# A hybrid attention and recurrence block: the recurrence's values projected for row blocks 4 to 7 first, and two kinds of transfer tied behind the next copy

## The chip, the cores and the metric

The kernel runs on one core of one Trainium2 chip. The metric is the time of one execution on the device in microseconds (us), the median over several runs. A core has five engines that run their own instruction queues side by side: TensorE (PE) for matmuls, VectorE (DVE), ScalarE (ACT), GpSimd (POOL) and SyncE (SP), which here only issues transfers. DMA transfers are issued from the queues of ACT, SP and POOL, and an issue stands in its queue like any other instruction.

## The reference

Input x has 1024 rows of 1024 channels, in float32. What the block computes, cut to what matters:

```python
u = rmsnorm(x, norm1_g) @ w_in
q_sb, k_sb, v_sb, f_raw, i_hg, q_hg, g_hg, gate_sb, gate_hg = split(u)
o_sb = stick_breaking_attention(q_sb, k_sb, v_sb)      # 8 heads of 64, strictly causal
f = lb + (1 - lb) * sigmoid(f_raw)                     # forget gate, per channel
k_hg = (1 - lb) * sigmoid(-f_raw)
# recurrence, 4 heads of 128: S_t = diag(f_t) S_{t-1} + k_t v_t^T, o_t = S_t^T q_t
o_hg = hgrn2_chunkwise(silu(q_hg), k_hg, i_hg, log(f)) # i_hg: the values v_t
o_hg = rmsnorm(o_hg, hg_norm_g) * silu(g_hg)
merged = sigmoid(gate_sb + b) * (o_sb @ w_o_sb) + sigmoid(gate_hg + b) * (o_hg @ w_o_hg)
h = x + merged @ w_out
h = h + square(relu(rmsnorm(h, norm2_g) @ w_ff1)) @ w_ff2
return rmsnorm(h, final_g)
```

In the attention, weight A[t,s] is sigmoid(z_ts) times the product of (1 - sigmoid(z_tj)) over the positions j between s and t.

## The kernel before

Every float32 operand of a matmul is split into a high part (a cast on ACT, line 156) and a low part (a subtraction on DVE, line 161), and each product is made of three matmuls: high by high, high by low, low by high. In the program's names the letters h and l behind a tile's name are these parts (wih and wil are those of the weights wi). All matmuls come from line 128, transposes from line 131. SBUF holds a pool of 40 tiles ("slots") of 128 x 1024 that the stages take in turn, and PSUM gives eight banks.

A scheduler orders the instructions of each engine from the data dependences and a cost model; the program's text sets priorities (`open_block`) and not the final order. `after(ins, earlier)` gives it one more rule, that `ins` is issued behind `earlier`, without making it wait for that instruction's end by a semaphore. A stream `st` of projection work (each job is some hundred matmuls that don't depend on what is under way) is dealt out between the steps of the attention, and later of the recurrence, so that TensorE has work while ACT and DVE do theirs.

**Attention.** Per head, the query blocks of 128 rows run in the order 7, 0, 6, 1, 5, 2, 4, 3. For each, TensorE makes z, ACT two activations of it (rm at line 804, bt at 807), DVE a running sum (line 826) and a product, TensorE transposes the weights into pw, and ACT and DVE split them into wTh and wTl. `values(h, qc)` then multiplies two query blocks' weights with V into the bank po, and ACT copies po into a quarter of the tile osb (line 902). After the fourth quarter of a head, a DMA from POOL's queue adds the lower 64 partitions of osb to the upper (line 908). `keep_attended` stores the sum to the DRAM tensor od (line 919). It is called for one head in the course of a later `values` call of the next head, and the store is issued from ACT's queue wherever the scheduler has put it; the last head's store goes through SP's queue.

**Recurrence.** `i_job` projects the values i_hg of all four heads: for each of the eight row blocks tb (128 rows) 24 matmuls into a bank pji and a copy by ACT into half of a tile `val_t` (line 977). Tiles v0 and v1 hold blocks 0 to 3, v2 and v3 blocks 4 to 7. The rows of blocks 4 to 7 are needed in another order. So when an odd block of these has been copied, its tile is stored to DRAM (vd, line 980), and `turn_values` brings it back with its rows permuted by two DMAs (line 967), all from ACT's queue. The row blocks run from 0 to 7, and `turn_values` is called ahead of the next block's copy and once more in `hg_tail`.

`hg_tail(h)` makes head h's states: seven products of 128 x 128 (pkv, chunk c of 128 rows, v(c) being block c of the values), four in one bank and three in the next, then sums on DVE, then the outputs pho. For head 0 this follows the last block of the projection. sl and ksl are the recurrence's own products within a chunk, and pjf3 is the projection of the forget gate of head 3, which fills in there.

## Time and profile before

| | |
|---|---|
| timed runs | 1428.09, 1428.61, 1429.09 us; median 1428.61 |
| the profiled execution | 1429.28 us, of which 1427.5 from the first to the last instruction (the span) |
| granted TensorE clock, mean over the span | 0.997 of full speed |
| TensorE busy | 1411.4 us in 6848 matmuls, 99% of the span |
| VectorE, ScalarE, GpSimd busy | 1087.4, 684.2 and 146.6 us |
| stores of od on ACT's queue | 7, from 117.5 to 301.1 us, 2.9 to 3.1 us from issue to landing |
| projection of the recurrence's values | its copies by ACT start between 347.15 and 393.59 us |

The profile is one execution, taken by the hardware profiler. In the rows, `v<-pji` reads "tile v from tile pji"; numbers in names are left out there, so v stands for all four tiles of the values. PEld is TensorE's loading of the stationary operand, which runs beside its matmuls. `ACTq` and `DMA` rows are the issue of a transfer on ACT's queue and the transfer itself. Behind `[... <-X]` stands how long the engine was idle before the instruction, and what ended that. A wait for several semaphores is put down to the one that came last. The granted clock is the share of full speed at which TensorE was allowed to run.

### The profile page before, as it was taken

The numbers are of one execution on the slowest core, as the hardware profiler recorded it, in microseconds if no ns is written. First come the engines' busy times: TensorE is split into PE (matmuls) and PEld (weight loads), VectorE is DVE, ScalarE is ACT, GpSimd is POOL, SyncE is SP. The second block draws the span as 40 slices with busy tenths as digits, with TensorE's granted clock in tenths as the row PEclk, the third lists the DMA queues.
The fourth block names the chain that finished last, engine by engine and source line by source line (L and its number), as shares of the span: only waits on it lengthen the run. The fifth ranks groups of instructions, "written<-read, shape, count | busy, mean of one in ns | idle before, by whom it ended". The sixth has DMA issues, their size and how long they took to land.

```text
span 1427.5 us, 18779 instructions
## 1 busy us (share of the span) xinstructions
PE 1411.4 (99%) x6848; PEld 1186.3 (83%) x6848; DVE 1087.4 (76%) x1494; ACT 684.2 (48%) x1181; POOL 146.6 (10%) x340
## 2 busy tenths in 40 slices
PE   9999999999989999999999999999999999999998
PEld 7888888888878888888888888888888888888886
DVE  7579989888557888797787897766666658668765
ACT  6366676764233555333334764454444443524343
POOL 3012223210011021000000300000000000000042
PEclk9999999999999999999999999999999999999999
DMA  7124446535115785465486405443446974776825
GB/s 240 27 67 126 112 99 105 92 82 148 42 61 156 250 198 186 155 196 173 131 300 218 177 31 199 161 145 136 146 158 233 344 269 148 279 275 237 277 102 180
DMA packets 162597, 237.72 MB, mean 167 GB/s; under 512 B 26268, under 2 KB 93384, under 8 KB 162504
## 3 DMA queue, kind: packets, MB, share of 16 engines
q1 hardware_dynamic: 145480, 190.37, 39.9%
q0 software_dynamic: 11584, 34.61, 9.9%
q10 hardware_dynamic: 5440, 11.54, 2.3%
q8 instruction: 54, 0.88, 0.3%
q14 instruction: 39, 0.32, 0.1%
HBM read 168.32 MB, written 66.06 MB: 164 GB/s over the span
## 4 chain that ended last, share of the span: by engine, by line
PE 96%; DMA 1%; DVE 1%; ACT 1%; POOL 0%; issue 0%; SPq 0%; ACTq 0%; DVEq 0%
PE pm L128 21%; PE pX L128 9%; PE pW L128 6%; PE pY L128 6%; PE pjqk L128 5%; PE pga L128 4%; PE gX L128 4%; PE gY L128 4%; PE pjq L128 3%; PE pys L128 3%; PE pji L128 3%; PE pyh L128 3%; PE pjv L128 3%; PE pjf L128 3%; PE po L128 3%; PE z L128 2%
## 5 line engine op out<-in xcount | busy, mean ns | idle before, releaser
L156 ACT CAST whid<-w 128x1024 fp32r<-128x1024 f32 x30 | 31.6, 1052 | 154.5 <-PE pm L128 86.2
L826 DVE TENSOR_TENSOR_SCAN rm<-rm,bits 128x511 f32<-128x511 f32 (+7 forms) x72 | 87.3, 1220 | 17.5 <-ACT rm L804 17.5
L128 PE MATMUL pm<-wlod,sh 128*128 128x512 f32 x240 | 93.5, 390 | 0.0
L128 PE MATMUL pm<-whid,sh 128*128 128x512 f32 x240 | 93.4, 389 | 0.0
L128 PE MATMUL pm<-whid,sl 128*128 128x512 f32 x240 | 93.4, 389 | 0.0
L128 PE MATMUL pm<-th,sl 128*128 128x512 f32 (+1 forms) x210 | 81.3, 387 | 0.0
L128 PE MATMUL pm<-tl,sh 128*128 128x512 f32 (+1 forms) x210 | 81.3, 387 | 0.0
L128 PE MATMUL pm<-th,sh 128*128 128x512 f32 (+1 forms) x210 | 81.3, 387 | 0.0
L161 DVE TENSOR_TENSOR wlod<-w,whid 128x1024 fp32r<-128x1024 f32 x30 | 36.7, 1224 | 53.8 <-ACT whid L156 53.8
L161 DVE TENSOR_TENSOR sl<-sa,sh 128x1024 fp32r<-128x1024 f32 x56 | 68.3, 1220 | 0.1
L156 ACT CAST wTh<-pw 128x512 fp32r<-128x512 f32 (+2 forms) x96 | 43.9, 488 | 41.2 <-PE pw L131 38.9
L2143 POOL TENSOR_SCALAR fss<-fss 128x1 f32<-128x1 f32 x8 | 4.5, 560 | 562.0 <-ACT fsc L2138 561.5
L156 ACT CAST sh<-sa 128x1024 fp32r<-128x1024 f32 x56 | 57.2, 1044 | 6.3 <-DMA sa<-ad 6.3
L128 PEld LDWEIGHTS pm<-wlod,sh 128*128 128x128 f32 x240 | 45.0, 188 | 9.7 <-DVE wlod L161 0.4
L128 PEld LDWEIGHTS pm<-whid,sh 128*128 128x128 f32 x240 | 45.1, 188 | 9.4
L128 PEld LDWEIGHTS pm<-whid,sl 128*128 128x128 f32 x240 | 45.1, 188 | 9.4
L161 DVE TENSOR_TENSOR wTl<-pw,wTh 128x512 fp32r<-128x512 f32 (+2 forms) x96 | 49.9, 546 | 3.8 <-ACT wTh L156 3.8
L169 DVE TENSOR_TENSOR bt<-bt,rm 128x511 f32<-128x511 f32 (+7 forms) x72 | 49.1, 685 | 4.0
L804 ACT ACTIVATE rm<-z 128x511 f32<-128x511 f32 (+4 forms) x96 | 48.2, 502 | 7.1 <-DMA osb<-osb 2.5
L128 PE MATMUL pX<-sqh,t1l 128*128 128x512 f32 x128 | 49.9, 390 | 0.0
L128 PE MATMUL pX<-sql,t1h 128*128 128x512 f32 x128 | 49.9, 390 | 0.0
L128 PE MATMUL pX<-sqh,t1h 128*128 128x512 f32 x128 | 49.8, 389 | 0.0
(930 smaller groups left out, 4443.2 us busy)
## 6 DMA issues: line engine op xcount, KB each, us to landing
w<-in_w_ff_dram SPq DMA_DIRECT2D x72, 512.0 KB, 4.7
sa<-ad SPq DMA_DIRECT2D x56, 512.0 KB, 7.1
ad<-a SPq DMA_DIRECT2D x32, 256.0 KB, 4.6
ad<-s SPq DMA_DIRECT2D x16, 512.0 KB
tw<-in_w_out_dram POOLq DMA_DIRECT2D x24, 256.0 KB, 4.9
pr<-pd SPq DMA_DIRECT2D x10, 512.0 KB, 5.5
x<-in_x_dram SPq DMA_DIRECT2D x8, 512.0 KB, 10.0
xnl<-xnh POOLq DMA_DIRECT2D x8, 512.0 KB, 6.2
```

Of the source, the lines that this page charges most:

```text
L128: return pe(nc.tensor.matmul(*a, **k))
L156: hi_last[0] = after(in_turn("act", nc.scalar.copy(dst, src)), hi_behind[0])
L161: nc.vector.tensor_tensor(out=dst, in0=src, in1=hi.bitcast(F32), op=ALU.subtract),
L169: return nc.vector.tensor_tensor(out=out, in0=a, in1=b, op=ALU.mult)
L804: nc.scalar.activation(rm[:, s0 + c0 - 1 : s0 + m - 1], z[:, c0:m], AF.Sigmoid, scale=-0.125)
L826: sc = nc.vector.tensor_tensor_scan(out=rr, data0=rr, data1=bits[:, 1024 - nk + a : 1024 - nk + b][:, ::-1], initial=rm[:, b : b + 1] if i ...
L2143: nc.gpsimd.tensor_scalar(out=ssq, in0=ssq, scalar1=1.0 / D, scalar2=EPS, op0=ALU.mult, op1=ALU.add)
```

## The change

The row blocks of the recurrence's values are projected in the order 4, 5, 6, 7, 0, 1, 2, 3. `turn_values` is called behind each block's copy and ties its two transfers behind that copy, so a pair's return is issued after the copy of the next block; the call in `hg_tail` is gone. Likewise `keep_attended` is called behind each copy of osb, and the store of the head that was summed before is tied behind that copy, the first one of the next head; the counter of calls is gone.

```diff
--- before.py
+++ after.py
@@ -899,24 +899,22 @@
         if to_come.get(h) is None:
             to_come[h] = NT // 2
             osb[h] = slot(f"osb{h}")
-        nc.scalar.copy(osb[h][:, qc * 256 : (qc + 1) * 256], po)
+        kept = nc.scalar.copy(osb[h][:, qc * 256 : (qc + 1) * 256], po)
         to_come[h] -= 1
-        if summed and summed[0][1] == 1:
-            keep_attended()
-        summed[:] = [(a, n + 1) for a, n in summed]
+        keep_attended(behind=kept)
         if to_come[h] == 0:
             nc.gpsimd.dma_start(osb[h][0:DHS, :], osb[h][DHS:P, :], accum_op=ALU.add)
-            summed.append((h, 0))
+            summed.append(h)
 
     summed = []
 
-    def keep_attended(queue=nc.scalar):
+    def keep_attended(queue=nc.scalar, behind=None):
         while summed:
-            h = summed.pop()[0]
+            h = summed.pop()
             pair, r = h // 2, (h % 2) * DHS
             if r == 0:
                 od[pair] = dram(f"od{pair}", [P, 1024])
-            queue.dma_start(od[pair][r : r + DHS, :], osb.pop(h)[0:DHS, :])
+            after(queue.dma_start(od[pair][r : r + DHS, :], osb.pop(h)[0:DHS, :]), behind)
 
 
     hg, ohg = {}, {}
@@ -955,32 +953,32 @@
             if upto is not None:
                 Unit.split(self, upto)
 
-    val_t, stored = [], []
+    val_t, stored = {}, []
     u_i = wide_unit("wi", W_IN, C_I, HGW)
     u_i.__class__ = ByParts
 
-    def turn_values():
+    def turn_values(behind):
         while stored:
             t, vd = stored.pop()
             rows = vd.rearrange("(n g r) c -> n g r c", g=16, r=2)[:, ::-1]
             for r in range(2):
-                nc.scalar.dma_start(t[r::2], rows[:, :, r])
+                after(nc.scalar.dma_start(t[r::2], rows[:, :, r]), behind)
 
     def i_job():
         unit = u_i
 
         def ep(ps, tb):
+            pair = tb // 2
             if tb % 2 == 0:
-                val_t.append(slot(f"v{tb // 2}"))
+                val_t[pair] = slot(f"v{pair}")
             cs = slice(tb % 2 * 512, (tb % 2 + 1) * 512)
-            turn_values()
-            nc.scalar.copy(val_t[-1][:, cs], ps)
+            turn_values(nc.scalar.copy(val_t[pair][:, cs], ps))
             if tb >= NT // 2 and tb % 2:
                 vd = dram(f"vd{tb}", [P, 1024])
-                nc.scalar.dma_start(vd, val_t[-1])
-                stored.append((val_t[-1], vd))
-
-        return st.add([unit], lambda: token_steps("pji", unit, xn, range(NT), ep, n=HGW))
+                nc.scalar.dma_start(vd, val_t[pair])
+                stored.append((val_t[pair], vd))
+
+        return st.add([unit], lambda: token_steps("pji", unit, xn, (*range(4, NT), *range(4)), ep, n=HGW))
 
     def silu_epilogue(h, key):
         def ep(ps, half):
@@ -1203,7 +1201,6 @@
             nc.scalar.copy(ktk[:, half * 512 : half * 512 + n * P], pk[:, : n * P])
         yield
         st.finish(j_i)
-        turn_values()
         open_block("main")
         for half in range(2):
             pkv = bank(f"pkv{h}_{half}")
```

TensorE at the end of the projection of the values, before: pji_7 is the bank of block 7, pkv0_0 and pkv0_1 are the two banks of head 0's state products, v0 to v3 the tiles of the values (numbers behind the last underscore are running numbers).

```order
L128 MATMUL pji_7_4202<-wih3_3856,xnl13_575 128x512
L128 MATMUL pkv0_0_4256<-v0_3913,pp0_2863 128x128 x2
L128 MATMUL pkv0_0_4256<-v1_3990,pp0_2863 128x128 x2
L128 MATMUL pkv0_1_4265<-v2_4084,pp0_2863 128x128 x2
...
L128 MATMUL pkv0_1_4265<-v3_4198,pp0_2863 128x128
L128 MATMUL sl1_5_4301<-q1_3332,ksl1_5_4299 128x128 x4
L128 MATMUL pho0_0_4325<-v0_3913,sc0_3764 128x128 x2
```

The same place on TensorE now:

```order
L128 MATMUL pji_3_4206<-wih3_3856,xnl03_254 128x512
L128 MATMUL pkv0_0_4256<-v0_4090,pp0_2865 128x128 x2
L128 MATMUL pkv0_0_4256<-v1_4204,pp0_2865 128x128
L128 MATMUL pkv0_1_4265<-v2_3913,pp0_2865 128x128
L128 MATMUL pkv0_0_4256<-v1_4204,pp0_2865 128x128
L128 MATMUL pkv0_1_4265<-v2_3913,pp0_2865 128x128
L128 MATMUL pkv0_1_4265<-v3_3992,pp0_2865 128x128
L128 MATMUL pjf3_0_4286<-xnh00_229,wf3h0_4272 128x512
```

Before, 24 matmuls of pjf3 stand between the sixth product and the seventh, which reads v3; now the seventh follows the sixth, and the product that reads the block projected last (the second one with v1) is the fifth.

ScalarE at the end of the same projection, before: the copies of the blocks, the stores of a pair (vd5, vd7) and its return.

```order
L977 COPY v2_4084<-pji_5_4086 128x512
L980 DMA vd5_4143<-v2_4084 128x1024
L967 DMA v2_4084<-vd5_4143 64x1x1024 x2
L1063 COPY ksl1_3_4209<-k1_3092 128x2x32x8
L977 COPY v3_4198<-pji_6_4145 128x512
L1063 COPY ksl1_4_4233<-k1_3092 128x2x16x16
L1063 COPY ksl1_5_4299<-k1_3092 128x2x8x32
L977 COPY v3_4198<-pji_7_4202 128x512
L980 DMA vd7_4252<-v3_4198 128x1024
L967 DMA v3_4198<-vd7_4252 64x1x1024 x2
```

ScalarE at the same copies of blocks 6 and 7 now, with the block that follows:

```order
L975 COPY v3_3992<-pji_6_3967 128x512
L965 DMA v2_3913<-vd5_3953 64x1x1024 x2
...
L975 COPY v3_3992<-pji_7_4010 128x512
L978 DMA vd7_4048<-v3_3992 128x1024
L975 COPY v0_4090<-pji_0_4050 128x512
L965 DMA v3_3992<-vd7_4048 64x1x1024 x2
L1201 COPY pp0_2865<-pk0_0_4104 128x512
```

The return of the second pair was the last of the projection and is now behind the fifth of the eight copies, with three blocks still to come; the return of the first pair moved behind the copy of block 6.

ScalarE in head 3 of the attention, before: the store od1 of head 2, the casts of weights wTh that feed TensorE's po, and the cast wqk6h of a block of projection weights.

```order
L156 CAST wTh3_0_0_2021<-pw3_0_0_2025 128x128
L919 DMA od1_2167<-osb2_1763 64x1024
L804 ACTIVATE rm3_5_2032<-z3_5_0_2033 128x511
...
L989 ACTIVATE q0_1957<-pjq0_1_1962 128x512
L992 COPY qx0_1_2051<-pjq0_1_1962 128x512
L156 CAST wTh3_3_0_1969<-pw3_6_0_2056 128x4x128
L156 CAST wTh3_3_4_1971<-pw3_6_1_2063 128x3x128
L804 ACTIVATE rm3_2_2072<-z3_2_0_2073 128x383
L807 ACTIVATE bt3_2_2071<-z3_2_0_2073 128x383
L156 CAST wqk6h0_2080<-wqk6r0_1867 128x1024
```

The same place now, as far as the store:

```order
L156 CAST wqk6h0_2080<-wqk6r0_1867 128x1024
L987 ACTIVATE q0_1957<-pjq0_1_1962 128x512
L990 COPY qx0_1_2051<-pjq0_1_1962 128x512
L156 CAST wTh3_3_0_1969<-pw3_6_0_2056 128x4x128
L156 CAST wTh3_3_4_1971<-pw3_6_1_2063 128x3x128
L804 ACTIVATE rm3_2_2072<-z3_2_0_2073 128x383
L807 ACTIVATE bt3_2_2071<-z3_2_0_2073 128x383
L156 CAST wTh3_0_0_2021<-pw3_1_0_2094 128x2x128
L902 COPY osb3_2116<-po3_3_2099 128x256
L917 DMA od1_2118<-osb2_1763 64x1024
```

The store has moved behind the first copy of osb3, and the cast wqk6h from behind the two wTh casts to ahead of them.

## The prediction

> **What bounds the kernel now.** I read the page's busy times first, then TensorE's waits, then the chain and the stretch table around the one large wait, and last the timelines of ScalarE (ACT), VectorE (DVE) and TensorE (PE) wherever the order of instructions changes. The busy times are the page's first part.

> ```profile
> PE 1411.4 (99%) x6848; PEld 1186.3 (83%) x6848; DVE 1087.4 (76%) x1494; ACT 684.2 (48%) x1181; POOL 146.6 (10%) x340
> ```

> TensorE works in 1411.4 of the 1427.5 us of the span. The number of its matmuls does not change, so a gain can only come from the 16.1 us in which it is idle, or from matmuls that ran at less than the full clock. TensorE's waits (us in total, times, longest) say how much of that idle time has a name.

> ```profile
> PE pkv L128 <- DMA v<-vd: 4.9, 1, 4.9
> PE warm L128 <- POOL ident masks.py:199: 2.2, 1, 2.2
> PE po L128 <- DVE wTl L161: 0.7, 2, 0.4
> ```

> The second is the program's start, which the change does not touch. The first is in the middle of the program: the state products of recurrence head 0 wait for the values that come back from DRAM. The chain of waits around it (start, length in us) shows how it arises.

> ```profile
> 393.59 0.59 ACT v L977
> ...
> 394.21 2.60 DMA vd<-v
> ...
> 396.83 0.53 ACTq L967
> ...
> 397.41 7.84 DMA v<-vd
> ...
> 405.29 0.80 PE pkv L128 x2
> ```

> The last block of values is copied out of PSUM at 393.59, stored (2.60 us), brought back with its rows turned (7.84 us), and the seventh state product can start at 405.29. The round trip takes 11.7 us from the copy; TensorE has other work for it only until 400.35. The table by stretches has the busy time of PE, PEld, DVE, ACT and POOL, then the granted clock, DMA share and GB/s.

> ```profile
> 393.40:400.35 6.95, 6.95 (x37) 5.66 (x35) 2.39 (x7) 0.59 (x1) 0.00 (x0) 1.00 0.27 97
> 400.35:405.25 4.90, 0.00 (x0) 0.00 (x0) 1.03 (x2) 1.09 (x2) 0.00 (x0) 0.93 0.21 76
> 405.25:411.40 6.15, 6.11 (x26) 5.96 (x27) 3.56 (x6) 1.60 (x9) 0.00 (x0) 0.50 0.01 3
> 411.40:420.00 8.60, 8.60 (x51) 7.54 (x50) 5.51 (x10) 4.46 (x16) 1.23 (x2) 1.00 0.00 0
> ```

> TensorE does nothing for 4.90 us, and the 6.15 us behind that run at half the clock. The idle stretch therefore costs twice: itself, and half of the stretch behind it.

> **The change part by part.** *The order of the value blocks.* Blocks 4 to 7 are projected first, so the two round trips begin at the fourth copy of the eight at the latest. ACT's copies of the eight blocks lie at these places today (the fourth to the sixth shown, and the last):

> ```profile
> 366.06 0.59 ACT L977 COPY v<-pji 128x512 f32<-128x512 f32 x1
> 371.43 0.59 ACT L977 COPY v<-pji 128x512 f32<-128x512 f32 x1 [4.78 <-PE pji L128]
> 378.59 0.59 ACT L977 COPY v<-pji 128x512 f32<-128x512 f32 x1 [4.39 <-PE pji L128]
> 381.83 1.70 ACTq L967 DMA_DIRECT2D v<-vd  x2
> 393.59 0.59 ACT L977 COPY v<-pji 128x512 f32<-128x512 f32 x1 [2.21 <-PE pji L128]
> ```

> The new last transfer is issued behind the fifth copy: 371.43 + 0.59 + 1.70 for both issues + 7.84 lands at 381.6. The state products start at 393.40 (row below), so there are 11.8 us to spare, and the 4.90 us of idle time go: **-4.94** (the timeline gives this gap as 4.94). What is late next is the copy of the last block, now block 3, which TensorE needs for the state product of chunk 3. In the new order that product is the fifth of the seven:

> ```profile
> 393.40 1.50 PE L128 MATMUL pkv<-v,pp 128*128 128x128 f32 x12
> ```

> Twelve records for six products give 0.25 us a product, so the fifth starts at 394.4; the copy ends at 393.59 + 0.59 = 394.18. It is hidden with 0.2 us to spare, and 0.6 us is all it could cost. The idle stretch gone, the clock should stay up: 6.15 us at 0.50 contain 3.07 us of full-speed work, so **-3.07**. The gap's row has 0.93 instead of 1.00, that is 0.7 us at half clock in which nothing ran; had work lain there too, the price would be 3.4. The timed runs (1428.09, 1428.61, 1429.09) lie up to 1.2 us below the profiled 1429.28, so a run may carry as little as 1.9. I take 3.07 and keep 1.9 to 3.4. No stretch of the middle other than this one loses the clock.

> [...]

> *The transfers are tied behind the next copy.* On ACT's queue the two issues (1.70 us) now stand behind the third and the fifth copy, with casts and copies of the recurrence queued behind them. The most urgent of these is a cast whose row is followed here by its first matmul:

> ```profile
> 361.35 0.62 ACT L156 CAST sl_h<-sl_x 128x512 fp32r<-128x512 f32 x1 [0.69 <-ACT sc L1129]
> 379.75 0.39 PE L128 MATMUL sl<-sl_h,ones 128*128 128x512 f32 x1
> ```

> It has 17.8 us of room against 1.7 of delay: nothing. If that cover were gone, it would be 1.7 us once.

> *The attention output store is tied behind the next copy of values.* In head 4 the store stands on ACT's queue too early today: it waits for the DMA that adds the two halves, and everything on ACT waits behind it. The chain's row, then ACT's and TensorE's:

> ```profile
> 203.58 5.05 DMA osb<-osb
> ```
> ```profile
> 208.71 0.45 ACTq L919 DMA_DIRECT2D od<-osb  x1
> 209.21 0.60 ACT L804 ACTIVATE rm<-z 128x511 f32<-128x511 f32 x1 [2.49 <-DMA osb<-osb]
> ```
> ```profile
> 213.70 0.36 PE L128 MATMUL po<-wTh,V 128*128 128x256 f32 x1
> 214.45 0.38 PE L128 MATMUL po<-wTl,V 128*128 128x256 f32 x1 [0.38 <-DVE wTl L161]
> 214.67 0.28 PE L128 MATMUL po<-wTh,V 128*128 128x256 f32 x1
> ```

> ACT stands 2.49 us for the sum. Of that, TensorE feels the step from 213.70 to 214.45: 0.75 us where the same matmuls elsewhere follow at 0.12 (182.79 to 182.90 below). Behind the next copy the sum has long landed, so **-0.6**, with 0 to 0.65 as bounds. The clock did not react to this short gap.

> *What the store's new place moves beside it.* In head 3 the scheduler now puts the split of a weight block (a cast on ACT, a subtraction on DVE) ahead of work that TensorE waits for closely. Today's rows of ACT, DVE and TensorE:

> ```profile
> 180.60 1.04 ACT L156 CAST wTh<-pw 128x512 fp32r<-128x512 f32 x2
> 182.20 1.15 ACT L156 CAST wqk6h<-wqk6r 128x1024 fp32r<-128x1024 f32 x1
> ```
> ```profile
> 181.30 0.67 DVE L169 TENSOR_TENSOR q<-qx,q 128x512 f32<-128x512 f32 x1
> 181.88 1.15 DVE L161 TENSOR_TENSOR wTl<-pw,wTh 128x512 fp32r<-128x512 f32 x2
> 183.81 1.22 DVE L161 TENSOR_TENSOR wqk6l<-wqk6r,wqk6h 128x1024 fp32r<-128x1024 f32 x1
> ```
> ```profile
> 181.75 0.28 PE L128 MATMUL po<-wTh,V 128*128 128x256 f32 x1
> 182.79 0.28 PE L128 MATMUL po<-wTl,V 128*128 128x256 f32 x1
> 182.90 0.28 PE L128 MATMUL po<-wTh,V 128*128 128x256 f32 x1
> ```

> The first of the two wTh casts ends after half of their 1.04, at about 181.1, and moves back by the cast's 1.15, less about 0.1 of overlap with its neighbour, to 182.2. TensorE's first po matmul also moves up by one and would start at 181.5: a wait of 0.7. The first wTl, about 182.5 today, moves back by the 1.22 of wqk6l to about 183.7; TensorE has three of the four matmuls that fill 181.75 to 182.79 today, 0.23 each, behind 182.2; it would start at 182.9 and waits 0.8. Together **+1.5**. Nothing, if ACT and DVE have idle time ahead that absorbs it, is the lower bound; 1.15 + 1.22 = 2.4 is the upper.

> *Buffers held longer.* All seven stores on ACT's queue leave later, and each keeps a buffer until it has landed. The tile's rows, the one wait that such stores end today, and one example of the distance:

> ```profile
> L919 ACTq DMA_DIRECT2D od<-osb x7: 452/453/539, 117.5 to 301.1; - x7
> ...
> DMA to landing us min/median/max: 2.9/3.0/3.1
> ```
> ```profile
> POOL bt L808 <- DMA od<-osb: 12.2, 2, 6.3
> ```
> ```profile
> 117.51 0.54 ACTq L919 DMA_DIRECT2D od<-osb  x1
> ...
> 123.13 0.37 ACT L902 COPY osb<-po 128x256 f32<-128x256 f32 x1 [0.31 <-PE po L128]
> ```

> The first store moves from 117.51 behind the copy at 123.13, 5.6 us or more later. The waits of POOL (GpSimd) are two clears of attention tiles, and none of TensorE's named waits comes from them; by my reading of the timelines, the next users of these buffers have at least 3 us of room. I cost it at nothing; without that room it is the third rival.

> *Sum*: -4.94 - 3.07 - 0.6 + 1.5 = -7.1. On the profiled execution (1429.28; its span 1427.5 plus 1.8 around it) that gives 1422.2. The median of the timed runs is 0.67 below it, and the same -7.1 gives **1421.5 us**.

> **The rivals.** *The idle time goes, but little else*: the clock's part is 1.9 instead of 3.07 and head 3 costs its full 2.4, with nothing won in head 4. Then -4.94 - 1.9 + 2.4 = -4.4, or 1424.2; with no clock gain at all 1424.6 even at head 3's 1.5 and head 4's -0.6 (-4.94 + 0.9 = -4.0). For it speaks that the clock is known from one profiled execution; against it, that the 0.50 follows the idle stretch directly. It stays faster.

> *The wait only moves*: the state products wait for something else for about as long, such as the recurrence's copies delayed on ACT or a return transfer that crawls. The return would have to take 7.84 + 11.8 = 19.6 us. Then only -0.6 + 1.5 remain: 1429.5. The 27% DMA share of the stretch and ACT's 48% speak against it.

> *Slower through held buffers*: the two clears that wait for an od store (12.2 us in all) wait 5.6 us longer each, and that delay reaches TensorE through the attention tiles behind them. Then -7.1 + 11.2 = +4.1, or 1432.7. It decides once new idle time of TensorE exceeds 7.1 us, and shows as slower beyond 10. Against it speaks that a clear which waits 6.3 us today leaves no trace in TensorE's waits.

> **How the numbers follow.** Forecast 0.79, first rival 0.08, second 0.06, third 0.07. The forecast's own bounds are -4.94 - 3.4 - 0.65 + 0 = -9.0 (1419.6) and, by the first rival, -4.0 (1424.6); rounded outward for the spread of timed runs the range is 1419.3 to 1425.0. It leaves out the last two rivals. About 0.2% (2.9 us) is what a measurement of this kernel can tell from no change: faster means below 1425.75. That takes the forecast and nearly all of the first rival, 0.86; within 0.2% 0.07, slower 0.07.

> **What would show it.** In the changed kernel's waits, the pkv line with v<-vd is gone; the seven products run in one piece, with pjf matmuls directly behind; the granted clock reads 1.00 in every stretch of the middle. ACT no longer waits for the sum of osb in head 4, and the step at po there is 0.12. Head 3 shows a new wait of po for wTh or wTl of 0.7 to 0.8 us each. A wait of TensorE over 1 us between 90 and 340 us, a clear on POOL ending just before such a wait, or a stretch at half clock would make the prediction wrong.

## The result and the profile after

The changed kernel takes 1421.14 us, median of 6 runs (1421.01 to 1421.59), against 1428.85 for the kernel before, also 6 runs (1427.43 to 1429.5). The ratio is 0.9948, interval 0.9935 to 0.996: 7.7 us less. The forecast was 1421.5.

The profiled execution has a span of 1419.4 us, 8.1 less than before. The page's busy times, and below them TensorE's waits (us in total, times, longest):

```profile
PE 1408.7 (99%) x6848; PEld 1183.7 (83%) x6848; DVE 1087.5 (77%) x1494; ACT 684.5 (48%) x1181; POOL 142.0 (10%) x340
```
```profile
PE warm L128 <- POOL ident masks.py:199: 2.2, 1, 2.2
PE po L128 <- DVE wTl L161: 0.7, 2, 0.4
PE pjqk L128 <- DVE xnl L351: 0.3, 1, 0.3
```

The line of pkv with v<-vd is gone. TensorE's busy time fell as well, by 2.7 us with the same 6848 matmuls, which fits matmuls that no longer run at half the clock (the prediction had 3.07 for them). The table by stretches, with the same limits as before from the second row on, shows both. Its columns are again busy PE, PEld, DVE, ACT and POOL, then the granted clock, DMA share and GB/s.

```profile
393.64:400.35 6.71, 6.71 (x42) 5.97 (x41) 4.16 (x11) 1.62 (x5) 0.00 (x0) 1.00 0.00 0
400.35:405.25 4.90, 4.90 (x30) 4.29 (x29) 1.03 (x2) 2.74 (x11) 0.52 (x2) 1.00 0.02 3
405.25:411.40 6.15, 6.15 (x41) 5.50 (x40) 5.40 (x9) 2.54 (x5) 0.71 (x1) 1.00 0.00 0
```

TensorE is busy throughout and the clock stands at 1.00. The stretch of 6.15 us now holds 41 matmul records instead of 26. The timelines of TensorE and ACT show the place itself:

```profile
393.64 1.77 PE L128 MATMUL pkv<-v,pp 128*128 128x128 f32 x14
395.16 0.48 PE L128 MATMUL pjf<-xnh,wf3h 128*128 128x512 f32 x1
```
```profile
371.67 0.59 ACT L975 COPY v<-pji 128x512 f32<-128x512 f32 x1 [4.85 <-PE pji L128]
371.73 1.08 ACTq L965 DMA_DIRECT2D v<-vd  x2
...
393.83 0.59 ACT L975 COPY v<-pji 128x512 f32<-128x512 f32 x1 [2.21 <-PE pji L128]
```

All 14 records of the seven state products run in one piece. The last return is issued from 371.73 on, 22 us ahead of them; from 380 to 386 us the profile shows no transfer at all, so it is back more than 13 us early. The copy of the last block ends at 394.42, and the product that reads it, the fifth, was due at 393.64 + 4 x 0.25 = 394.64: 0.2 us to spare, as forecast.

In head 3 of the attention, ACT, DVE and TensorE now read:

```profile
177.56 0.60 ACT L804 ACTIVATE rm<-z 128x511 f32<-128x511 f32 x1 [0.28 <-PE z L128]
...
179.06 1.07 ACT L156 CAST wqk6h<-wqk6r 128x1024 fp32r<-128x1024 f32 x1
...
180.95 1.02 ACT L156 CAST wTh<-pw 128x512 fp32r<-128x512 f32 x2
```
```profile
180.68 1.20 DVE L161 TENSOR_TENSOR wqk6l<-wqk6r,wqk6h 128x1024 fp32r<-128x1024 f32 x1
...
182.40 1.15 DVE L161 TENSOR_TENSOR wTl<-pw,wTh 128x512 fp32r<-128x512 f32 x2
```
```profile
182.34 0.39 PE L128 MATMUL pjqk<-xnh,wqk5l 128*128 128x512 f32 x1
183.14 0.39 PE L128 MATMUL po<-wTl,V 128*128 128x256 f32 x1 [0.41 <-DVE wTl L161]
```

The split of wqk6 stands ahead, as the order had it, and po has a new wait for wTl. From 182.34 to 183.14 there are 0.80 us where one matmul of this shape takes 0.23, so TensorE lost about 0.57 at this point. The po matmuls on either side of it add about 0.1 each: the first starts 0.24 behind the transposes ahead of it instead of 0.13, and the one behind the wait follows after 0.22 instead of 0.11. In head 4, ACT's rm now waits for TensorE's z alone, the store stands behind the copy of osb, and the step is gone:

```profile
207.80 0.60 ACT L804 ACTIVATE rm<-z 128x511 f32<-128x511 f32 x1 [0.19 <-PE z L128]
...
216.84 0.45 ACTq L917 DMA_DIRECT2D od<-osb  x1
```
```profile
214.59 0.36 PE L128 MATMUL po<-wTh,V 128*128 128x256 f32 x1
214.79 0.28 PE L128 MATMUL po<-wTl,V 128*128 128x256 f32 x1
214.91 0.28 PE L128 MATMUL po<-wTh,V 128*128 128x256 f32 x1
```

Comparing the start of the same TensorE work in both traces gives a running account: the changed kernel is 0.1 us late ahead of head 3 and 0.9 behind it, 0.2 behind head 4, and 7.75 early once the outputs pho of recurrence head 0 have begun. It ends 8.1 early; nothing of that size happens anywhere else.

### The profile page after: what moved, and what is told of

The parts are those of the page before. It is cut to its first block, busy times and chain, and to the rows that moved or that the text cites. A ratio compares the mean times of both kernels' runs of the same rounds, so it can differ in the third digit from the quotient of the medians.

```text
span 1419.4 us, 18788 instructions
## 1 busy us (share of the span) xinstructions
PE 1408.7 (99%) x6848; PEld 1183.7 (83%) x6848; DVE 1087.5 (77%) x1494; ACT 684.5 (48%) x1181; POOL 142.0 (10%) x340
## 4 chain that ended last, share of the span: by engine, by line
PE 97%; ACT 1%; DVE 1%; POOL 0%; DMA 0%; issue 0%; SPq 0%; DVEq 0%; ACTq 0%
PE pm L128 21%; PE pX L128 9%; PE pW L128 6%; PE pY L128 6%; PE pjqk L128 6%; PE pga L128 4%; PE gX L128 4%; PE gY L128 4%; PE pjf L128 3%; PE pys L128 3%; PE pji L128 3%; PE pyh L128 3%; PE pjq L128 3%; PE pjv L128 3%; PE po L128 3%; PE z L128 2%
## 5 line engine op out<-in xcount | busy, mean ns | idle before, releaser
L156 ACT CAST whid<-w 128x1024 fp32r<-128x1024 f32 x30 | 31.6, 1054 | 154.3 <-PE pm L128 86.0
L128 PE MATMUL pm<-whid,sh 128*128 128x512 f32 x240 | 93.4, 389 | 0.0
L128 PE MATMUL pm<-wlod,sh 128*128 128x512 f32 x240 | 93.4, 389 | 0.0
L128 PE MATMUL pm<-whid,sl 128*128 128x512 f32 x240 | 93.4, 389 | 0.0
L128 PE MATMUL pm<-tl,sh 128*128 128x512 f32 (+1 forms) x210 | 81.3, 387 | 0.0
L128 PE MATMUL pm<-th,sl 128*128 128x512 f32 (+1 forms) x210 | 81.3, 387 | 0.0
L128 PE MATMUL pm<-th,sh 128*128 128x512 f32 (+1 forms) x210 | 81.3, 387 | 0.0
L161 DVE TENSOR_TENSOR wlod<-w,whid 128x1024 fp32r<-128x1024 f32 x30 | 36.6, 1222 | 55.7 <-ACT whid L156 55.7
L161 DVE TENSOR_TENSOR sl<-sa,sh 128x1024 fp32r<-128x1024 f32 x56 | 68.2, 1217 | 0.1
L156 ACT CAST wTh<-pw 128x512 fp32r<-128x512 f32 (+2 forms) x96 | 43.8, 485 | 41.6 <-PE pw L131 40.7
L156 ACT CAST sh<-sa 128x1024 fp32r<-128x1024 f32 x56 | 57.2, 1046 | 7.3 <-DMA sa<-ad 7.3
L161 DVE TENSOR_TENSOR wTl<-pw,wTh 128x512 fp32r<-128x512 f32 (+2 forms) x96 | 49.9, 546 | 4.3 <-ACT wTh L156 4.1
L128 PEld LDWEIGHTS pm<-whid,sl 128*128 128x128 f32 x240 | 45.1, 188 | 9.4
L128 PEld LDWEIGHTS pm<-wlod,sh 128*128 128x128 f32 x240 | 45.0, 187 | 9.4
L128 PEld LDWEIGHTS pm<-whid,sh 128*128 128x128 f32 x240 | 45.1, 188 | 9.3
L169 DVE TENSOR_TENSOR bt<-bt,rm 128x511 f32<-128x511 f32 (+7 forms) x72 | 49.0, 684 | 3.4
L804 ACT ACTIVATE rm<-z 128x511 f32<-128x511 f32 (+4 forms) x96 | 48.0, 500 | 5.5 <-PE z L128 2.9
L128 PE MATMUL pX<-sqh,t1l 128*128 128x512 f32 x128 | 49.9, 390 | 0.0
L128 PE MATMUL pX<-sql,t1h 128*128 128x512 f32 x128 | 49.9, 390 | 0.0
L128 PE MATMUL pX<-sqh,t1h 128*128 128x512 f32 x128 | 49.8, 389 | 0.0
```

The source lines that it names most:

```text
L128: return pe(nc.tensor.matmul(*a, **k))
L156: hi_last[0] = after(in_turn("act", nc.scalar.copy(dst, src)), hi_behind[0])
L161: nc.vector.tensor_tensor(out=dst, in0=src, in1=hi.bitcast(F32), op=ALU.subtract),
L169: return nc.vector.tensor_tensor(out=out, in0=a, in1=b, op=ALU.mult)
L804: nc.scalar.activation(rm[:, s0 + c0 - 1 : s0 + m - 1], z[:, c0:m], AF.Sigmoid, scale=-0.125)
```

## The experiments

The theory: the idle time at pkv and the half clock behind it are one loss, and the block order removes both. The stores' new place wins about 0.66 us in head 4 and loses about 0.8 in head 3. The rivals: the clock fell for another reason; or the moved stores carry part of the gain. Each experiment's own kernel before, on the same chip, had a median between 1428.45 and 1428.81. The diffs below leave out lines that only carry a change through, such as a changed default value or index.

**The two halves of the change apart.** The first kernel has the new `i_job`, `turn_values` and `hg_tail`, with the old `values` and `keep_attended`. The second is the reverse.

> Only the order of the value blocks and the tied returns are taken over; the attention output stores stand as before the change. Theory (the idle 4.9 us and the half clock behind it are one loss, and the block order alone removes both): 8.0 us below the kernel before, about 1420.8; head 4 keeps its step of 0.75 us at po, head 3 has none. Rival 1 (the clock falls for another reason): 4.9 us below, about 1423.9, with a stretch at half clock somewhere. Rival 2 (the moved stores carry part of the gain): less than 7 us below.

> Only the attention output stores are tied behind the next copy; the value blocks run from 0 to 7 as before. Theory: head 3 loses about 0.8 us and head 4 wins 0.66, so +0.1 against the kernel before, within 0.5 us of it; the wait of 4.9 us at pkv and the half clock behind it stay. Rival 2 (the stores carry part of the gain): 1 us or more below the kernel before.

Block order alone: 1421.36 us (1421.21 to 1421.95), ratio 0.995 (0.9937 to 0.9962), 7.45 below its kernel before. Its profile has no wait at pkv, and no stretch at half clock between the start and the end of the program: its mean granted clock is 0.999, as that of the changed kernel, against 0.997 before; its span is 8.0 below the first one's. Stores alone: 1428.51 (1427.58 to 1428.85), ratio 0.9997 (0.9988 to 1.0006), no difference that can be told. Its waits and its stretches show the old picture:

```profile
PE pkv L128 <- DMA v<-vd: 4.8, 1, 4.8
```
```profile
400.45:405.25 4.80, 0.00 (x0) 0.00 (x0) 1.03 (x2) 1.08 (x2) 0.00 (x0) 0.85 0.21 77
405.25:410.60 5.35, 5.34 (x25) 5.34 (x26) 3.56 (x6) 1.02 (x4) 0.00 (x0) 0.50 0.02 3
410.60:415.00 4.40, 4.40 (x25) 3.79 (x25) 1.59 (x4) 2.23 (x11) 1.24 (x2) 1.00 0.00 0
```

So the block order carries the gain, and the stores add nothing in sum. The first rival falls: its 4.9 us lie outside the interval (5.4 to 9.0 us below), and no stretch at half clock is left. The interval alone would not exclude the second rival's limit of 7 us. What does is that the block order alone comes within about 0.2 us of the whole change (1421.36 and 1421.14), and that the stores alone change nothing that can be told. The running account says where the stores' two parts went: with the stores alone it loses 0.8 us in head 3 and wins 0.65 in head 4; with the block order alone it moves by 0.1 us at most in these heads and by 8.0 at the gap.

**The tie of the returns.** The changed kernel, with the returns placed ahead of the next copy:

```diff
-            turn_values(nc.scalar.copy(val_t[pair][:, cs], ps))
+            turn_values()
+            nc.scalar.copy(val_t[pair][:, cs], ps)
```

> As the changed kernel, but the returns are not tied behind the next copy: they stand ahead of it on ScalarE's queue, behind the store of their own pair, which they wait for there. TensorE's order is that of the changed kernel. Theory (only the order of the blocks matters; ScalarE has idle time for the two waits of 2.6 us): within 0.4 us of the changed kernel. Rival (the tie keeps ScalarE free, and the waits would reach TensorE): 1 to 5 us slower than the changed kernel, with a new wait of TensorE between 350 and 395 us.

1421.17 us (1421.02 to 1421.51), the same as the changed kernel. If ACT waits for the store here, none of it reaches TensorE, whose waits are those of the changed kernel (the start 2.2 us, po 0.7, pjqk 0.3, none at pkv); in this block order the tie itself is worth nothing.

**Another way around the wait.** The kernel before, each block stored and returned by itself (a pair's tile is now taken when the first block of the pair comes, which is no change in this order):

```diff
-            if tb >= NT // 2 and tb % 2:
-                vd = dram(f"vd{tb}", [P, 1024])
-                nc.scalar.dma_start(vd, val_t[-1])
-                stored.append((val_t[-1], vd))
+            if tb >= NT // 2:
+                vd = dram(f"vd{tb}", [P, 512])
+                nc.scalar.dma_start(vd, val_t[-1][:, cs])
+                stored.append((val_t[-1][:, cs], vd))
```

> The kernel before with its block order 0 to 7, but each block of 4 to 7 is stored and returned by itself (256 KB, not the pair's 512 KB): the seventh product waits for block 6 alone, which is copied at 386.3 and should be back at 395 to 397; it stands directly behind the sixth product, at 394.9. Theory (what costs is that the last block's round trip stands in TensorE's way; any way around it gives the gain back): a gap of 0 to 2 us without a loss of clock, 6 to 8 us below the kernel before. Rival (twice as many transfers cost as much as they save, or a new wait for the last copy): within 2 us of the kernel before.

1422.0 us, ratio 0.9955 (0.9943 to 0.9968), but between 1421.35 and 1423.44. In its profile, which was the fastest of the five, all seven products again run in one piece at 1.00. Most of the gain can thus be had with the old order. What varies from run to run was not recorded; the return of block 6 is issued from 389.25 us on, and the products start at 393.66, so a late transfer would show in the time, where the changed kernel has over ten microseconds to spare. That this is the reason for the spread is not shown.

**How the clock answers to a gap.** Three kernels make the gap shorter or longer. In the changed kernel, block 3 goes last, so that the last return is issued behind the last copy:

```diff
-token_steps("pji", unit, xn, (*range(4, NT), *range(4)), ep, n=HGW)
+token_steps("pji", unit, xn, (0, 1, 2, 4, 5, 6, 7, 3), ep, n=HGW)
```

> Block order 0, 1, 2, 4, 5, 6, 7, 3: the last return is issued behind the last copy, about 394.5, and lands at about 403.3, where TensorE has other work only until about 399.5; a gap of 3 to 4 us comes back, shorter than the 4.9 before. Theory with a fixed price (any such gap halves the clock behind it): 3.5 + 3.1 = 6.6 us above the changed kernel, about 1427.7. Rival (the clock reacts only to longer gaps): 3.5 above it, about 1424.6, and full clock behind the gap.

In the kernel before, each pair takes another trip:

```diff
-                stored.append((val_t[-1], vd))
+                vd2 = dram(f"vx{tb}", [P, 1024])
+                nc.scalar.dma_start(vd2, vd)
+                stored.append((val_t[-1], vd2))
```

> The kernel before, but each pair takes a second trip from DRAM to DRAM ahead of its return, some 3 to 5 us longer: the gap at pkv grows from 4.9 to 8 to 10 us. Theory (the clock's price has a fixed top of half of 6.8 us, whatever the gap): the gap's growth and at most 0.4 us more, 3 to 5.5 us above the kernel before, and the stretch at half clock in the records that lies beside work no longer than 6.9 us. Rival (the price grows with the gap: as long at half clock as idle): one and a half times the growth, 4.5 to 8 us above.

And in the kernel with single blocks, the order ends with block 6:

```diff
-token_steps("pji", unit, xn, range(NT), ep, n=HGW)
+token_steps("pji", unit, xn, (0, 1, 2, 3, 4, 5, 7, 6), ep, n=HGW)
```

> As the run with single blocks, but block 6 is projected last (0 to 5, 7, 6), so that the seventh product waits for a single block's round trip from 393.6: back at 400.5 to 403, with other work until 400.3. A gap of 0.5 to 2.5 us, shorter than any so far. Theory from the run with one block behind (the clock falls once the idle part of one stretch of 3.4 us is large, 2.4 us there): for a gap under 2 us no stretch at half clock, 6 to 7.5 us below the kernel before; for more, one such stretch of 3.4 us, up to 1.7 us more. Rival (each gap costs half its length again): 1.5 times the gap, in every run alike.

The stretches (same columns) of the gap and of what follows it, for block 3 last, then for the extra trip, then for block 6 last:

```profile
399.40:402.10 2.70, 0.01 (x1) 0.01 (x1) 0.00 (x0) 0.00 (x0) 0.00 (x0) 0.95 0.18 74
402.10:405.25 3.15, 3.15 (x13) 2.96 (x13) 1.66 (x4) 0.59 (x3) 0.00 (x0) 0.50 0.00 0
405.25:412.00 6.75, 6.75 (x42) 5.99 (x41) 2.81 (x6) 3.81 (x15) 1.23 (x2) 1.00 0.01 2
```
```profile
400.50:409.90 9.40, 0.00 (x0) 0.02 (x1) 1.03 (x2) 1.19 (x2) 0.00 (x0) 0.78 0.17 56
409.90:416.00 6.10, 6.09 (x26) 5.93 (x27) 3.38 (x6) 1.62 (x9) 0.00 (x0) 0.50 0.01 3
416.00:420.00 4.00, 4.00 (x23) 3.46 (x22) 1.96 (x4) 1.67 (x8) 1.23 (x2) 1.00 0.00 0
```
```profile
400.55:402.85 2.30, 0.03 (x2) 0.04 (x1) 0.00 (x0) 0.00 (x0) 0.00 (x0) 1.00 0.18 69
402.85:409.00 6.15, 6.15 (x41) 5.61 (x42) 2.79 (x7) 3.66 (x15) 1.24 (x2) 1.00 0.01 3
```

Beside the times:

| kernel | gap in the profile, us | work at half clock behind it, us | median, us (range, runs) |
|---|---|---|---|
| changed kernel | none | none | 1421.14 (1421.01 to 1421.59, 6) |
| block 6 last | 2.27 | none | 1425.38 (1423.64 to 1427.63, 9) |
| block 3 last | 2.70 | 3.15 | 1425.2 (1424.21 to 1425.97, 9) |
| before | 4.94 | 6.1 | 1428.85 (1427.43 to 1429.5, 6) |
| extra trip | 9.45 | 6.1 | 1433.57 (1433.15 to 1434.31, 5) |

The extra trip lengthens the gap by 4.51 us and the time by 5.1 against its own kernel before (1428.46), while the work at half clock stays as long: in these two profiles the price of the clock does not grow with the gap, and the running account has the extra trip lose 4.6 us at this place, about the growth of the gap alone. The rival's stated 4.5 to 8 us holds the measured 5.1 too, but one and a half times the measured growth would be 6.8, more than any of the five runs shows (1434.31 is 5.9 above).

Block 3 last came back with 2.70 us of gap, not 3.5, and lost the clock for 3.15 us. So neither forecast was right for the profiled run: this shorter gap lost the clock, at about half the price (1.6 us, not 3.1). It did not in every run. The nine times fall into two groups: four from 1424.21 to 1424.33 with a mean clock of 0.998 or 0.999, as in the kernels without a gap, and five from 1425.20 to 1425.97 at 0.997. The middles of the groups lie 1.65 us apart, which is the price that the profile shows (half of 3.15 is 1.6). In the four, then, the same kernel very probably kept its clock, as the rival said (about 1424.6), and the median of 1425.2 stands for neither group.

In the profile of block 6 last, a gap of 2.27 us left the clock alone. But its nine times spread over 4 us with mean clocks from 0.997 to 0.999, so this is one outcome among several. Half of one stretch of 3.4 us at half clock, 1.7 us, would not span 4 us, so the gap itself probably varies too. The forecast of "6 to 7.5 us below" failed: it was 3.1 below by the medians.

**The stores, and a version that beats both.** In the first kernel only the store that head 4 waited for is tied, the others as before; in the second, all but head 2's store, which cost head 3 its time, are tied.

```diff
-        keep_attended(behind=kept)
+        if summed and summed[0][1] == 1:
+            keep_attended()
+        if summed and summed[0][0] == 3:
+            keep_attended(behind=kept)
+        summed[:] = [(a, n + 1) for a, n in summed]
```

> Block order and returns as after the change, but of the stores only that of head 3 (issued in head 4) is tied; the others stand where they did before. Theory: the gain in head 4 without the loss in head 3, so 8.0 + 0.66 = 8.7 us below the kernel before, 0.6 to 1.0 below the changed kernel. Rival (the loss of head 3 comes from elsewhere than the store's place): equal to the changed kernel within 0.3 us, with a step at po in head 3.

```diff
-        keep_attended(behind=kept)
+        if summed and summed[0] == 2 and to_come[h] == NT // 2 - 2:
+            keep_attended()
+        elif not summed or summed[0] != 2:
+            keep_attended(behind=kept)
```

> The changed kernel, with one store (of head 2, issued in head 3) put back where the scheduler had it before; the other stores and the returns stay tied. Theory (the whole loss of head 3 comes from this one store's place): the step of about 0.8 us in head 3 is gone and the gain in head 4 stays, 0.6 to 0.9 us below the changed kernel, about 1420.5, as in the run with one store tied. Rival (the other five tied stores cost or bring something too): more than 0.3 us away from that run's 1420.61.

> The changed kernel unaltered, beside the run with head 2's store free on the same chip: about 1421.1, 0.6 to 0.9 above it. Rival: within 0.2 us of it.

One store tied: 1420.61 us (1420.59 to 1420.77), ratio to before 0.9944 (0.9931 to 0.9956). All but head 2's tied: 1420.53 (1420.38 to 1420.86), ratio 0.9945 (0.9933 to 0.9958), beside 1421.35 (1421.22 to 1421.56) for the changed kernel on the same chip: 0.82 less, with no overlap. TensorE's timeline of the second has neither the step in head 3 nor that in head 4:

```profile
182.59 0.40 PE L128 MATMUL pjqk<-xnl,wqk5h 128*128 128x512 f32 x1
182.82 0.28 PE L128 MATMUL po<-wTl,V 128*128 128x256 f32 x1
...
213.72 0.36 PE L128 MATMUL po<-wTh,V 128*128 128x256 f32 x1
213.92 0.28 PE L128 MATMUL po<-wTl,V 128*128 128x256 f32 x1
```

Both versions agree within 0.1 us, so the other five stores cost and bring nothing in sum. The one place in head 3 is the change's whole loss.

## Why the prediction was right, step by step

The forecast was 7.1 us, and 7.7 were measured. The difference is about what the prediction charged too much for head 3. That the forecast time of 1421.5 lies only 0.4 from the result is a little luck: the three times it started from have a median of 1428.61, and all six a median of 1428.85.

**The idle time, -4.94.** Right: the wait at pkv is gone, nothing took its place, and the seventh product follows the sixth.

**The clock, -3.07.** Right for the profiled execution, where the two together come to 8.0 between the same points. By medians, 7.71 less 4.94, with +0.8 and -0.66 taken into account, leaves 2.9. The lower bound of 1.9, from timed runs up to 1.2 us below the profiled one, rested on a spread that was too narrow: the kernel before ranges over 2.2 us in all its runs and block 6 last over 4.0, while the kernels whose last return is back long before it is needed stay within 0.8, and the times of block 3 last fall into two groups 1.65 us apart. So the price probably varies from run to run; that is an inference from the times, as each kernel has one profile. A gap of 4.9 us that costs no clock at all was seen in no profile and fits no run: without any loss the kernel before would take about 1426 us (an estimate: 1421.14 + 4.94, less the stores' 0.1), and the lowest of all its times is 1427.43.

**Head 4, -0.6.** Right: the account goes from +0.9 to +0.2, and ACT no longer waits for the sum.

**Head 3, +1.5.** The mechanism was right and the size was not: it cost 0.8. The step that failed is "the first of the two wTh casts ... moves back by the cast's 1.15": it moved by 0.35 (180.60 to 180.95). ACT's timeline of the kernel before has the reason ahead of it:

```profile
177.61 0.45 ACTq L919 DMA_DIRECT2D od<-osb  x1
178.17 0.60 ACT L804 ACTIVATE rm<-z 128x511 f32<-128x511 f32 x1 [1.00 <-PE z L128]
```

The store of od that left this place had occupied ACT's queue directly ahead of rm, and rm now starts 0.61 earlier, at 177.56. I counted what the store's move put ahead of TensorE's work and not what it took away. DVE gains as much: its running sum starts at 179.01 instead of 179.63, so the first wTl moves back by 0.5 and not by 1.22. The first po then waits about 0.1 instead of 0.7, the second 0.57 instead of 0.8, and another 0.1 is lost behind it: 0.8 together.

**Held buffers, nothing.** Right. The waits on these stores changed their places:

```profile
  POOL wTl L862: 7.8, 1
  POOL bt L808: 3.2, 1
  POOL wTh L862: 0.5, 1
```

They are 11.5 us in all, as against 12.2, all on POOL. None reaches TensorE: between 90 and 340 us the running account moves in heads 3 and 4 only.

## What to carry to other kernels

Where a round trip ends a stage, look at which block is asked for last and which is available earliest: starting the blocks that must travel first cost nothing here and hid the trip. Here a gap on TensorE cost more than its length, because the clock behind it counted too: 4.94 us of idle time and about 3 us more for the work at half clock, and 2.70 us and 1.6 more in the profile with block 3 last, though not in every run of that kernel. So a short idle time in an otherwise full engine is worth looking for. When a transfer's issue is moved on a queue, count what it frees at the old place and what the scheduler slides into the hole, and check each moved store alone: here one of seven ate the profit of another.
